# Seven of eight row-tile pairs in seven products, with the sums of weight blocks on POOL

## The chip, the cores and the metric

The kernel runs on one core of one Trainium2 chip. The metric is the device time of one execution in microseconds, the median of the runs shown. The engines are named as in the profile: PE (matrix products; PEld its weight loads), DVE (elementwise on vectors), ACT (activations and copies), POOL (GpSimd), SP (whose queue issues nearly all DMAs).

## The reference

The program is a two-layer decoder trunk over 256 tokens of 2048 features, in float32. Layer 0 mixes tokens with an mLSTM, layer 1 with an RG-LRU; behind each mixer comes a SwiGLU feed-forward block, which is the part that the change touches:

```python
D_MODEL = 2048; SEQ = 256; DEPTH = 2
D_FF = ((8 * D_MODEL // 3 + 255) // 256) * 256        # 5632

def swiglu(x, w_in, w_out):
    g, u = jnp.split(x @ w_in, 2, axis=-1)
    return (jax.nn.silu(g) * u) @ w_out

    h = x
    for layer in range(DEPTH):
        h = h + mixer(rms_norm(h, norm_mix[layer]), ...)
        h = h + swiglu(rms_norm(h, norm_ffn[layer]), ffn_w_in[layer], ffn_w_out[layer])
    return rms_norm(h, norm_final)
```

`ffn_w_in[layer]` is 2048 x 11264, `ffn_w_out[layer]` 5632 x 2048.

## The kernel before

**Split numbers.** A float32 product is made from three matmuls on a faster type (`fp32r`): every operand is split into a rounded part hi and a rest lo = x - hi, and hi*hi + hi*lo + lo*hi is accumulated in PSUM. For each weight block ACT makes hi by a cast and DVE makes lo by a subtraction whose two inputs (the raw weights and hi) lie in SBUF (`split`, `halves`, L267 to L269 and L243, L244 elsewhere). `product` (L818 to L821) issues the three matmuls, each 128 x 128 by 128 x 512.

**Blocks and pairs.** A feed-forward layer goes over 11 column blocks `j` of 512 gate and 512 up columns. Within a block it goes over eight pairs `p` of row tiles (2 x 128 rows of the weights). A pair of row tiles, two column halves (gate and up) and two token blocks of 128 form a 2 x 2 by 2 x 2 block product. The plain form takes eight products (24 matmuls). For the pairs in `SEVENS` a Strassen form with seven products (21 matmuls) is used, with results gathered in seven PSUM banks named P1, P2, Q3, Q5, P7, Q6, P4. It needs three raw weight blocks (B21, B11, B22, the tile called x) and four sums of weight blocks (T1, T3, T2, T4, the tile called t). In block 0 the pairs in `BOTH` are plain too.

**One pair of weights** (`pairs`, L293 to L318): SP issues two 512 KB loads into a raw tile of four 512-wide blocks. For a seven-product pair DVE makes the sums in a single buffer `sum` (L312: two blocks at once, 1024 wide; L315 and L316: one block each). ACT casts x (`whix`, 1536 wide) and t in two halves (`whit`, 1024 wide), DVE makes `wlox` and `wlot`. Three raw buffers and three hi and three lo buffers take turns; x and t of a pair take one hi and one lo buffer each, a plain pair takes one of each.

**Output.** The result of a block goes through L853 to L868 (copies, sums of banks, SiLU, product of gate and up; every bank must be read before the next block restarts it), is transposed into the banks P7 and Q6, and is multiplied with `ffn_w_out` in eight pieces of 12 matmuls. From block 1 on, `between` (L889 on) puts one such piece into each pair, a few products before its end, for the block before. Its weights (`rawo`, `whio`, `wloo`) are loaded by SP and split like the others, in 16 half blocks of 512 columns as eight pieces of 1024.

**Order.** Every engine runs its own queue in order. The order within a queue comes from the program's order and from `high_priority(offset=AHEAD)`, which moves weight splits ahead of what the program has just written; `pool_of(...).tile(..., tag=...)` gives a buffer, and whoever takes it again waits for its last reader.

Of the kernel before, what the change touches and what calls it, by code (L numbers as in the profile page):

```python
# [26 lines left out]
BIG = 1e30  # L27
AHEAD = 1000

SEVENS = (1, 2, 3, 4, 5, 6)  # L30

BOTH = (1, 2, 3, 4)

# [2 lines left out]
    ("P1", "A11", "B11"), ("P2", "A12", "B21"), ("Q3", "A3", "B22"),  # L36
    ("Q5", "A5", "T1"), ("P7", "A7", "T3"), ("Q6", "A6", "T2"), ("P4", "A22", "T4"),
)
SEVEN = ("A12", "A22", "A11", "A5", "A7", "A6", "A3")


@with_exitstack
def kernel(
# [38 lines left out]
    def pool_of(key):  # L82
        return pools[key][0]
# [73 lines left out]
    for i in range(9):  # L157
        nc.tensor.matmul(pwarm[:, 0:P], lhsT=ones, rhs=ones, start=True, stop=True)
    mhalf = const.tile([P, 2], F32, name="mhalf")
    nc.vector.memset(mhalf, -0.5)  # L160
    mask = const.tile([P, P], F32, name="mask")
    nc.gpsimd.memset(mask, 0.0)
    nc.gpsimd.affine_select(
        out=mask, in_=mask, compare_op=ALU.is_ge, fill=BIG, base=0,
        pattern=[[1, P]], channel_multiplier=-1,
    )


    par_src = [
# [55 lines left out]
    def stream(w, c0, nk, ncols=NB):  # L225
# [23 lines left out]


    PLACES = (
        "raw1", "raw2", "sum0", "rawo", "whio", "wloo", "wlo1", "whi1", "wlo2", "whi2", "raw0", "whi0", "wlo0",
    )
    turn, early = {}, {}

# [15 lines left out]
    def halves(name, src, n=4, step=4):  # L271

        hi, lo = four("whi", name, F32R, 3), four("wlo", name, F32R, 3)
        for i in range(0, n, step):
            at = slice(i, min(n, i + step))
            split(hi[:, at, :], lo[:, at, :], src[:, at, :])
        return [(hi[:, i, :], lo[:, i, :]) for i in range(n)]

    def stream4(w, c0, nk):

        wv = w.rearrange("(k p) n -> p k n", p=P)
        for kg in range(0, nk, 4):
            raw = four("raw", kg, F32, 3)
            for i in (0, 2):
                nc.sync.dma_start(raw[:, i:i + 2, :], wv[:, kg + i:kg + i + 2, c0:c0 + NB])
            with tc.high_priority(offset=AHEAD):
                both = halves(kg, raw)
            for i in range(4):
                yield kg + i, *both[i]

    def is_plain(j, p):
        return p not in SEVENS or j == 0 and p in BOTH

    def pairs(w, j, held):

        wv = w.rearrange("(k p) n -> p k n", p=P)
        for p in range(NK // 2):
            raw = four("raw", f"{j}_{p}", F32, 3)
            if held and j == 0 and p == 0:

                nc.vector.tensor_copy(raw[0:1, 0, 0:1], h[0:1, NT - 1, 2 * NB - 1:2 * NB])
            for i, c0 in enumerate((j * NB, FF + j * NB)):
                nc.sync.dma_start(raw[:, 2 * i:2 * i + 2, :], wv[:, 2 * p:2 * p + 2, c0:c0 + NB])
            if is_plain(j, p):
                with tc.high_priority(offset=AHEAD):
                    both = halves(f"{j}_{p}", raw)
                yield p, both
                continue

            with tc.high_priority(offset=AHEAD):  # L310
                t = four("sum", f"{j}_{p}", F32, 1)
                nc.vector.tensor_tensor(  # L312
                    t[:, 0:2, :], raw[:, 1:3, :], raw[:, 3:4, :].broadcast_to([P, 2, NB]), op=ALU.add
                )
                nc.vector.tensor_tensor(t[:, 2, :], t[:, 0, :], raw[:, 2, :], op=ALU.add)  # L315
                nc.vector.tensor_tensor(t[:, 3, :], t[:, 2, :], raw[:, 0, :], op=ALU.add)  # L316
                both = halves(f"x{j}_{p}", raw, 3) + halves(f"t{j}_{p}", t, step=2)
            yield p, dict(zip(("B21", "B11", "B22", "T1", "T3", "T2", "T4"), both))  # L318

# [45 lines left out]
    class Norm:  # L365
# [9 lines left out]
        def __init__(self, name, gain, bcast=False):  # L375
            self.name, self.gain, self.bcast, self.made = name, gain, bcast, []
            self.x = []
            self.ss = small.tile([P, NT, 4], F32, tag="ss", name=f"ss_{name}")

        def stats(self, q, blocks=range(NT)):  # L380
            for b in blocks:
                junk = self.scrap
                if junk is None:
                    junk = small.tile([P, NB], F32, tag="junk", name="junk", bufs=1)
                nc.scalar.activation(
                    junk, h[:, b, q * NB:(q + 1) * NB], AF.Square,
                    accum_out=self.ss[:, b, q:q + 1],
                )
# [47 lines left out]
        def finish(self):  # L436
            v = small.tile([P, NT], F32, tag="ms", name=f"ms_{self.name}")
            nc.vector.tensor_reduce(out=v, in_=self.ss, axis=mybir.AxisListType.X, op=ALU.add)
            nc.vector.tensor_scalar(out=v, in0=v, scalar1=1.0 / D, scalar2=EPS, op0=ALU.mult, op1=ALU.add)
            self.rstd = small.tile([P, NT], F32, tag="rstd", name=f"rstd_{self.name}")  # L440
            nc.gpsimd.tensor_tensor(self.rstd, v, mhalf[:, 0:NT], op=ALU.pow)
            if self.bcast:
                dg = small.tile([P, NT, P], F32, tag="dg", name=f"dg_{self.name}", bufs=1)
                for b in range(NT):
                    nc.vector.tensor_scalar_mul(dg[:, b, :], ident, self.rstd[:, b:b + 1])
                pb = misc(f"bc_{self.name}")
                nc.tensor.matmul(pb[:, 0:T], lhsT=ones, rhs=dg.rearrange("p b t -> p (b t)"), start=True, stop=True)
                self.bc = small.tile([P, T], F32, tag="rbc", name=f"rbc_{self.name}")
                nc.scalar.copy(self.bc, pb[:, 0:T])

    class NormPairs(Norm):


        def __init__(self, *args, **kw):
            super().__init__(*args, **kw)
            self.more = {}

        def pair(self, p):
            plain = p not in SEVENS
# [109 lines left out]
    def mlstm_mixer():  # L569
        mx = open_pool("mx", "mx", 2)  # L570
        if True:
            w = m_w_in[0]
            sel = mx.tile([H, H, P], F32R, name="sel", bufs=1)
            nc.gpsimd.tensor_copy(sel, ident[0:H, 0:H].unsqueeze(2).broadcast_to([H, H, P]))

            gw = mx.tile([P, NK, 2 * H], F32, name="gw", bufs=1)
            gwx = mx.tile([P, NK, 2, 2 * H], F32R, name="gwx", bufs=1)
            gsel = mx.tile([4 * H, 2 * H], F32, name="gsel", bufs=1)
# [132 lines left out]
            def head_out(j, a, vs, hn):  # L711
                hd = 2 * j + a
                for b in range(NT):
                    pv = misc(f"pv{hd}_{b}")
                    o = pv[:, 0:DV + 1]
                    if b == 0:
                        nc.tensor.matmul(o, lhsT=pw[hd][:, 0:P], rhs=vs[:, 0, a, :], start=True, stop=True)
                    else:
                        nc.tensor.matmul(o, lhsT=pw[hd][:, P:2 * P], rhs=vs[:, 0, a, :], start=True, stop=False)
                        nc.tensor.matmul(o, lhsT=pw[hd][:, 2 * P:3 * P], rhs=vs[:, 1, a, :], start=False, stop=True)  # L720
                    den = mx.tile([P, 4], F32, tag="den", name="den", bufs=4)
                    nc.vector.tensor_scalar(
                        out=den[:, 1:2], in0=pv[:, DV:DV + 1], scalar1=-1.0,
                        scalar2=ucol[:, 3 + b, hd:hd + 1], op0=ALU.mult, op1=ALU.max,
                    )
                    nc.vector.tensor_tensor(den[:, 0:1], pv[:, DV:DV + 1], den[:, 1:2], op=ALU.max)
                    nc.vector.reciprocal(den[:, 0:1], den[:, 0:1])
                    nc.vector.tensor_scalar_mul(hn[:, b, a, :], pv[:, 0:DV], den[:, 0:1])
                    junk = small.tile([P, NB], F32, tag="junk", name="junk", bufs=1)
                    nc.scalar.activation(junk[:, 0:DV], hn[:, b, a, :], AF.Square, accum_out=den[:, 1:2])  # L730
                    nc.vector.tensor_scalar(
                        out=den[:, 2:3], in0=den[:, 1:2], scalar1=1.0 / DV, scalar2=EPS,
                        op0=ALU.mult, op1=ALU.add,
                    )
                    nc.gpsimd.tensor_tensor(den[:, 3:4], den[:, 2:3], mhalf[:, 0:1], op=ALU.pow)
                    nc.gpsimd.tensor_scalar_mul(hn[:, b, a, :], hn[:, b, a, :], den[:, 3:4])
# [61 lines left out]
    def ffn(layer, n, nxt):  # L798
# [24 lines left out]
        def inner(j, between):  # L823
# [12 lines left out]
            for p, ops in pairs(w, j, layer == 1):  # L836
                if is_plain(j, p):

                    work = [
                        (c, n.plain(p, f)[a], ops[2 * side + f], p == NP - 1 and f == 1)  # L840
                        for c, side, a in (("Q5", 1, 1), ("P2", 0, 0), ("Q3", 1, 2), ("P4", 0, 1)) for f in range(2)
                    ]
                else:
                    seven = n.seven(p)
                    work = [
                        (c, seven[a], ops[b], p == SEVENS[-1] and c in ("P7", "P1", "Q6")) for c, a, b in PRODUCTS
                    ]
                for i, job in enumerate(work):
                    add(*job)
# [278 lines left out]
    class Final(Norm):  # L1128
# [9 lines left out]

        def mean(self, q, b, src):

            junk = small.tile([P, NB], F32, tag="junk", name="junk", bufs=1)
            nc.scalar.activation(junk, src, AF.Square, scale=D ** -0.5, accum_out=self.ss[:, b, q:q + 1])

        def scaled(self, q, b):
            cs = slice(q * NB, (q + 1) * NB)
# [63 lines left out]
```

## Time and profile before

| | before |
|---|---|
| median of 3 runs | 2085.85 us (2085.57 to 2086.32) |
| profiled execution | 2085.02 us, span 2083.2 us |
| granted PE clock | 0.999 |
| PE busy | 2069.3 us (99% of the span) |
| DVE busy | 1742.1 us (84%) |
| ACT busy | 1343.0 us (64%) |
| POOL busy | 43.2 us (2%) |
| sums on DVE (L312, L315, L316), 124 pairs | 151.5 + 85.3 + 85.2 us busy |
| DMA | 405.75 MB, mean 195 GB/s |

A row of the groups reads: line, engine, operation, out<-in by the program's names, shapes, count, then busy time in us, mean ns of one, and the idle time of the engine just before with what ended it. In a timeline row the first two numbers are the start and the duration in us, and what stands in brackets at its end is the engine's idle time before it. Durations of matmuls overlap, so PE's busy share says that it rarely stops, not what a matmul costs. The rest of the 2085 us outside the two feed-forward stages (about 395 to 1090 us and 1385 to 2083 us) is the mixers.

### The profile page before, as it was taken

What the parts mean: (1) busy time and instruction counts of PE and PEld (TensorE: products, weight loads), DVE (VectorE), ACT (ScalarE), POOL (GpSimd) and SP (SyncE); (2) the same over time, 40 slices, a digit from 0 to 9 for tenths busy, and PEclk for the clock granted to TensorE, in tenths of its full rate; (3) what the DMA queues carried; (4) which work ended last, traced back from release to release, by engine and by line L of the source; (5) the groups of instructions that cost most, each with busy time, mean ns of one, the idle gap of its engine ahead of it and who ended that gap; (6) DMA issues with size and microseconds to landing.
All of it is one profiled execution on the core that took longest, in us unless ns stands there. A gap on an engine that the chain in (4) does not pass through costs nothing.

```text
span 2083.2 us, 27536 instructions
## 1 busy us (share of the span) xinstructions
PE 2069.3 (99%) x10484; PEld 1752.6 (84%) x10484; DVE 1742.1 (84%) x1898; ACT 1343.0 (64%) x1627; POOL 43.2 (2%) x62
## 2 busy tenths in 40 slices
PE   9999999999999999999999999999999999999998
PEld 8988888887888888888889999888788888888886
DVE  6655556699999999999976787679999999999995
ACT  6344446566777676777764768556676776776774
POOL 0011110000000000000000000000000000000002
PEclk9999999999999999999999999999999999999999
DMA  7555656555665566565555665655556556566653
GB/s 229 171 162 177 178 181 222 190 173 200 206 215 198 192 216 208 200 216 192 185 179 161 192 187 189 219 207 181 201 204 222 195 186 208 201 211 212 202 188 135
DMA packets 211901, 405.75 MB, mean 195 GB/s; under 512 B 15080, under 2 KB 15800, under 8 KB 211640
## 3 DMA queue, kind: packets, MB, share of 16 engines
q1 hardware_dynamic: 211048, 402.92, 58.5%
q8 instruction: 82, 1.34, 0.3%
q10 hardware_dynamic: 720, 1.07, 0.1%
q14 instruction: 51, 0.42, 0.1%
HBM read 401.84 MB, written 2.10 MB: 194 GB/s over the span
## 4 chain that ended last, share of the span: by engine, by line
PE 93%; DVE 4%; ACT 1%; issue 1%; DMA 1%; POOL 0%; ACTq 0%; POOLq 0%; SPq 0%; DVEq 0%
PE P L820 7%; PE P L821 7%; PE out L819 7%; PE P L819 7%; PE out L821 7%; PE out L820 7%; PE Q L820 6%; PE Q L821 6%; PE Q L819 6%; PE po L330 3%; PE po L328 3%; PE po L329 3%; PE o L330 1%; PE v L328 1%; PE rec L347 1%; PE v L329 1%
## 5 line engine op out<-in xcount | busy, mean ns | idle before, releaser
L244 DVE TENSOR_TENSOR wlo<-raw,whi 128x1024 fp32r<-128x1024 f32 (+1 forms) x226 | 273.4, 1213 | 171.4 <-ACT whi L243 170.8
L243 ACT CAST whi<-raw 128x1024 fp32r<-128x1024 f32 (+1 forms) x226 | 234.7, 1043 | 196.7 <-PE po L330 43.3
L268 ACT CAST whit<-sum 128x1024 fp32r<-128x1024 f32 x248 | 255.1, 1052 | 145.0 <-DVE sum L316 79.4
L269 DVE TENSOR_TENSOR wlot<-sum,whit 128x1024 fp32r<-128x1024 f32 x248 | 297.2, 1220 | 20.0 <-ACT whit L268 20.0
L819 PE MATMUL out<-whio,hh 128*128 128x512 f32 x704 | 275.1, 391 | 0.1
L820 PE MATMUL out<-wloo,hh 128*128 128x512 f32 x704 | 274.1, 389 | 0.0
L821 PE MATMUL out<-whio,hh 128*128 128x512 f32 x704 | 273.9, 389 | 0.0
L269 DVE TENSOR_TENSOR wlox<-raw,whix 128x1536 fp32r<-128x1536 f32 x124 | 217.3, 1753 | 12.1 <-ACT whix L268 12.1
L268 ACT CAST whio<-rawo 128x1024 fp32r<-128x1024 f32 (+1 forms) x166 | 183.5, 1106 | 64.3 <-PE out L821 54.7
L269 DVE TENSOR_TENSOR wloo<-rawo,whio 128x1024 fp32r<-128x1024 f32 (+1 forms) x166 | 209.8, 1283 | 3.0 <-ACT whio L268 2.5
L268 ACT CAST whix<-raw 128x1536 fp32r<-128x1536 f32 x124 | 184.0, 1484 | 38.5 <-PE P L821 16.1
L938 ACT COPY h<-out 128x512 f32<-128x512 f32 x154 | 89.9, 584 | 126.1 <-PE out L821 125.8
L312 DVE TENSOR_TENSOR sum<-raw 128x1024 f32<-128x1024 f32 x124 | 151.5, 1222 | 7.0 <-DMA raw<-in_ffn_w_in_dram 2.6
L819 PEld LDWEIGHTS out<-whio,hh 128*128 128x128 f32 x704 | 132.1, 188 | 29.6 <-ACT out L927 1.8
L821 PEld LDWEIGHTS out<-whio,hh 128*128 128x128 f32 x704 | 132.1, 188 | 27.8
L820 PEld LDWEIGHTS out<-wloo,hh 128*128 128x128 f32 x704 | 132.2, 188 | 27.2
L269 DVE TENSOR_TENSOR wlo<-raw,whi 128x2048 fp32r<-128x2048 f32 x52 | 117.5, 2288 | 28.8 <-ACT whi L268 28.8
L268 ACT CAST whi<-raw 128x2048 fp32r<-128x2048 f32 x52 | 97.4, 1911 | 24.0 <-DMA raw<-in_ffn_w_in_dram 17.7
L819 PE MATMUL P<-whix,p_f 128*128 128x512 f32 x248 | 97.6, 399 | 1.8 <-ACT whix L268 1.8
L819 PE MATMUL Q<-whit,p_f 128*128 128x512 f32 x248 | 97.2, 392 | 0.8 <-ACT whit L268 0.8
L927 ACT COPY out<-h 128x512 f32<-128x512 f32 x156 | 91.9, 589 | 8.3 <-DVE h L936 6.7
L820 PE MATMUL P<-wlox,p_f 128*128 128x512 f32 x248 | 97.1, 391 | 0.2
(293 smaller groups left out, 5023.5 us busy)
## 6 DMA issues: line engine op xcount, KB each, us to landing
raw<-in_ffn_w_in_dram SPq DMA_DIRECT2D x352, 512.0 KB, 4.5
rawo<-in_ffn_w_out_dram SPq DMA_DIRECT2D x176, 512.0 KB, 4.9
raw<-in_m_w_in_dram SPq DMA_DIRECT2D x94, 512.0 KB, 3.7
raw<-in_r_w_in_dram SPq DMA_DIRECT2D x64, 512.0 KB, 4.4
raw<-in_m_w_out_dram SPq DMA_DIRECT2D x32, 512.0 KB, 3.8
raw<-in_r_w_out_dram SPq DMA_DIRECT2D x32, 512.0 KB, 4.3
gr<-in_r_gate_w_dram SPq DMA_DIRECT2D x8, 512.0 KB, 3.7
out_dram<-y SPq DMA_DIRECT2D x4, 512.0 KB, 3.0
```

The lines of the kernel that those rows point to most:

```text
L243: nc.scalar.copy(hi[:, i:i + step, 0:ncols], r)
L244: nc.vector.tensor_tensor(lo[:, i:i + step, 0:ncols], r, hi[:, i:i + step, 0:ncols].bitcast(F32), op=ALU.subtract)
L268: nc.scalar.copy(hi, src)
L269: nc.vector.tensor_tensor(lo, src, hi.bitcast(F32), op=ALU.subtract)
L312: nc.vector.tensor_tensor(t[:, 0:2, :], raw[:, 1:3, :], raw[:, 3:4, :].broadcast_to([P, 2, NB]), op=ALU.add)
L328: nc.tensor.matmul(o, lhsT=ah[:, bs], rhs=hi, start=(k == 0), stop=False)
L329: nc.tensor.matmul(o, lhsT=ah[:, bs], rhs=lo, start=False, stop=False)
L819: nc.tensor.matmul(o, lhsT=a[0], rhs=b[0], start=start, stop=False, **kw)
L820: nc.tensor.matmul(o, lhsT=a[0], rhs=b[1], start=False, stop=False, **kw)
L821: nc.tensor.matmul(o, lhsT=a[1], rhs=b[0], start=False, stop=stop, **kw)
L927: nc.scalar.copy(o, hs)
L938: nc.scalar.copy(hs, o)
```

## The change

`SEVENS` gains pair 7, so that only pair 0 stays plain from block 1 on. The sums move from DVE to POOL (`nc.gpsimd`), and are kept in half buffers of two blocks each: three of them take turns (`sums`; two in the place `sum0`, one in the new place `sum1`), and a pair uses two. Pair 7 goes through its seven products in the order `LAST`, since all seven banks now end there. The causal mask, the scratch tile `junk` and the tiles of the broadcast norm move into pools that are open only part of the time.

```diff
-SEVENS = (1, 2, 3, 4, 5, 6)
+SEVENS = (1, 2, 3, 4, 5, 6, 7)
...
+LAST = tuple(sorted(PRODUCTS, key=lambda c: ("P1", "Q6", "P7", "Q5", "P2", "Q3", "P4").index(c[0])))
...
     PLACES = (
-        "raw1", "raw2", "sum0", "rawo", "whio", "wloo", "wlo1", "whi1", "wlo2", "whi2", "raw0", "whi0", "wlo0",
+        "raw1", "raw2", "sum0", "rawo", "whio", "wloo", "wlo1", "whi1", "wlo2", "whi2", "raw0", "whi0", "wlo0", "sum1",
     )
...
-            split(hi[:, at, :], lo[:, at, :], src[:, at, :])
+            split(hi[:, at, :], lo[:, at, :], src[i // step] if isinstance(src, list) else src[:, at, :])
...
+    def sums(name):
+        at = turn.get("sum", 0)
+        turn["sum"] = (at + 1) % 3
+        return pool_of(f"sum{at // 2}").tile([P, 2, NB], F32, tag=f"sum{at}", name=f"sum{name}")
...
             with tc.high_priority(offset=AHEAD):
-                t = four("sum", f"{j}_{p}", F32, 1)
-                nc.vector.tensor_tensor(
-                    t[:, 0:2, :], raw[:, 1:3, :], raw[:, 3:4, :].broadcast_to([P, 2, NB]), op=ALU.add
-                )
-                nc.vector.tensor_tensor(t[:, 2, :], t[:, 0, :], raw[:, 2, :], op=ALU.add)
-                nc.vector.tensor_tensor(t[:, 3, :], t[:, 2, :], raw[:, 0, :], op=ALU.add)
+                t = [sums(f"{j}_{p}{i}") for i in range(2)]
+                nc.gpsimd.tensor_tensor(t[0], raw[:, 1:3, :], raw[:, 3:4, :].broadcast_to([P, 2, NB]), op=ALU.add)
+                nc.gpsimd.tensor_tensor(t[1][:, 0, :], t[0][:, 0, :], raw[:, 2, :], op=ALU.add)
+                nc.gpsimd.tensor_tensor(t[1][:, 1, :], t[1][:, 0, :], raw[:, 0, :], op=ALU.add)
                 both = halves(f"x{j}_{p}", raw, 3) + halves(f"t{j}_{p}", t, step=2)
...
                     seven = n.seven(p)
                     work = [
-                        (c, seven[a], ops[b], p == SEVENS[-1] and c in ("P7", "P1", "Q6")) for c, a, b in PRODUCTS
+                        (c, seven[a], ops[b], p == SEVENS[-1])
+                        for c, a, b in (LAST if p == SEVENS[-1] else PRODUCTS)
                     ]
```

**DVE, pairs 3 and 4 of a block in the first feed-forward layer.** Names end in the pair and a serial number. Before, the sums stand between the splits:

```order
L269 TENSOR_TENSOR wloo_8013<-rawo_8011,whio_8012 128x1024
L312 TENSOR_TENSOR sum_3_8047<-raw_3_8044 128x1024
L269 TENSOR_TENSOR wloo_8019<-rawo_8017,whio_8018 128x1024
L315 TENSOR_TENSOR sum_3_8047<-sum_3_8047,raw_3_8044 128x512
L269 TENSOR_TENSOR wlox_3_8052<-raw_3_8044,whix_3_8051 128x1536
L316 TENSOR_TENSOR sum_3_8047<-sum_3_8047,raw_3_8044 128x512
L269 TENSOR_TENSOR wlot_3_8056<-sum_3_8047,whit_3_8055 128x1024 x2
L312 TENSOR_TENSOR sum_4_8100<-raw_4_8097 128x1024
L315 TENSOR_TENSOR sum_4_8100<-sum_4_8100,raw_4_8097 128x512
L316 TENSOR_TENSOR sum_4_8100<-sum_4_8100,raw_4_8097 128x512
L269 TENSOR_TENSOR wlox_4_8105<-raw_4_8097,whix_4_8104 128x1536
```

The same place on DVE after the change:

```order
L265 TENSOR_TENSOR wlox_3_8183<-raw_3_8174,whix_3_8182 128x1536
L265 TENSOR_TENSOR wlot_3_8187<-sum_30_8177,whit_3_8186 128x1024
L265 TENSOR_TENSOR wlot_3_8187<-sum_31_8178,whit_3_8186 128x1024
L265 TENSOR_TENSOR wlox_4_8237<-raw_4_8228,whix_4_8236 128x1536
L265 TENSOR_TENSOR wlot_4_8241<-sum_40_8231,whit_4_8240 128x1024
L265 TENSOR_TENSOR wlot_4_8241<-sum_41_8232,whit_4_8240 128x1024
L265 TENSOR_TENSOR wloo_8263<-rawo_8261,whio_8262 128x1024
L265 TENSOR_TENSOR wloo_8269<-rawo_8267,whio_8268 128x1024
```

Only splits are left on DVE here, one behind the other, all of them with two inputs in SBUF.

**POOL, the first feed-forward layer.** Before, its queue goes from the norm's power (L441) straight to the next mixer:

```order
L735 TENSOR_TENSOR den<-den,mhalf 128x1
L736 TENSOR_SCALAR hn_2676<-hn_2676,den 128x256
L441 TENSOR_TENSOR rstd_f_3774<-ms_f_3771,mhalf 128x2
L1017 MEMSET rc_9188 128x4x3
L1017 MEMSET rc_9835 128x4x3
```

After the change the sums of all pairs stand in between, three operations a pair (`sum_30` and `sum_31` are the two half buffers of pair 3):

```order
L314 TENSOR_TENSOR sum_30_6659<-raw_3_6656 128x1024
L315 TENSOR_TENSOR sum_31_6660<-sum_30_6659,raw_3_6656 128x512
L316 TENSOR_TENSOR sum_31_6660<-sum_31_6660,raw_3_6656 128x512
L314 TENSOR_TENSOR sum_40_6713<-raw_4_6710 128x1024
L315 TENSOR_TENSOR sum_41_6714<-sum_40_6713,raw_4_6710 128x512
L316 TENSOR_TENSOR sum_41_6714<-sum_41_6714,raw_4_6710 128x512
```

The three additions of a pair moved from DVE's queue to POOL's, in the same order, each reading what the one before it wrote.

More of the change, by code (lines that the diff above doesn't have):

```diff
@@ L160 @@
     nc.vector.memset(mhalf, -0.5)
[L161 to L165, printed above, removed]
-    )
     par_src = [
@@ L310, in pairs @@
             with tc.high_priority(offset=AHEAD):
-                t = four("sum", f"{j}_{p}", F32, 1)
-                nc.vector.tensor_tensor(
-                    t[:, 0:2, :], raw[:, 1:3, :], raw[:, 3:4, :].broadcast_to([P, 2, NB]), op=ALU.add
-                )
-                nc.vector.tensor_tensor(t[:, 2, :], t[:, 0, :], raw[:, 2, :], op=ALU.add)
-                nc.vector.tensor_tensor(t[:, 3, :], t[:, 2, :], raw[:, 0, :], op=ALU.add)
+                t = [sums(f"{j}_{p}{i}") for i in range(2)]
+                nc.gpsimd.tensor_tensor(t[0], raw[:, 1:3, :], raw[:, 3:4, :].broadcast_to([P, 2, NB]), op=ALU.add)
+                nc.gpsimd.tensor_tensor(t[1][:, 0, :], t[0][:, 0, :], raw[:, 2, :], op=ALU.add)
+                nc.gpsimd.tensor_tensor(t[1][:, 1, :], t[1][:, 0, :], raw[:, 0, :], op=ALU.add)
                 both = halves(f"x{j}_{p}", raw, 3) + halves(f"t{j}_{p}", t, step=2)
@@ L378, in __init__, with junk @@
             self.ss = small.tile([P, NT, 4], F32, tag="ss", name=f"ss_{name}")
+        def junk(self):
+            return pool_of("x").tile([P, NB], F32, tag="junk", name="junk")
         def stats(self, q, blocks=range(NT)):
@@ L383, in stats @@
                 if junk is None:
-                    junk = small.tile([P, NB], F32, tag="junk", name="junk", bufs=1)
+                    junk = self.junk()
                 nc.scalar.activation(
@@ L442, in finish @@
             if self.bcast:
-                dg = small.tile([P, NT, P], F32, tag="dg", name=f"dg_{self.name}", bufs=1)
+                dg = pool_of("x").tile([P, NT, P], F32, tag="dg", name=f"dg_{self.name}")
                 for b in range(NT):
@@ L447, in finish @@
                 nc.tensor.matmul(pb[:, 0:T], lhsT=ones, rhs=dg.rearrange("p b t -> p (b t)"), start=True, stop=True)
-                self.bc = small.tile([P, T], F32, tag="rbc", name=f"rbc_{self.name}")
+                self.bc = pool_of("x").tile([P, T], F32, tag="rbc", name=f"rbc_{self.name}")
                 nc.scalar.copy(self.bc, pb[:, 0:T])
@@ L456, in __init__, with junk @@
             self.more = {}
+        def junk(self):
+            place, tag = ("c", "junk") if "c" in pools else ("rawo", "raw1")
+            return pool_of(place).tile([P, NB], F32, tag=tag, name="junk")
         def pair(self, p):
@@ L574, in mlstm_mixer @@
             nc.gpsimd.tensor_copy(sel, ident[0:H, 0:H].unsqueeze(2).broadcast_to([H, H, P]))
+            mask = mx.tile([P, P], F32, name="mask", bufs=1)
+            nc.gpsimd.memset(mask, 0.0)
+            nc.gpsimd.affine_select(
+                out=mask, in_=mask, compare_op=ALU.is_ge, fill=BIG, base=0,
+                pattern=[[1, P]], channel_multiplier=-1,
+            )
             gw = mx.tile([P, NK, 2 * H], F32, name="gw", bufs=1)
@@ L728, in head_out @@
                     nc.vector.tensor_scalar_mul(hn[:, b, a, :], pv[:, 0:DV], den[:, 0:1])
-                    junk = small.tile([P, NB], F32, tag="junk", name="junk", bufs=1)
-                    nc.scalar.activation(junk[:, 0:DV], hn[:, b, a, :], AF.Square, accum_out=den[:, 1:2])
+                    junk = mx.tile([P, DV], F32, tag="junk", name="junk", bufs=1)
+                    nc.scalar.activation(junk, hn[:, b, a, :], AF.Square, accum_out=den[:, 1:2])
                     nc.vector.tensor_scalar(
@@ L1139, in mean @@
         def mean(self, q, b, src):
-            junk = small.tile([P, NB], F32, tag="junk", name="junk", bufs=1)
-            nc.scalar.activation(junk, src, AF.Square, scale=D ** -0.5, accum_out=self.ss[:, b, q:q + 1])
+            nc.scalar.activation(self.junk(), src, AF.Square, scale=D ** -0.5, accum_out=self.ss[:, b, q:q + 1])
         def scaled(self, q, b):
```

## The prediction

> **What bounds the kernel now.** I read the page's busy shares first, then the chain that ended last, then busy time by stretches.
>
> ```profile
> PE 2069.3 (99%) x10484; PEld 1752.6 (84%) x10484; DVE 1742.1 (84%) x1898; ACT 1343.0 (64%) x1627; POOL 43.2 (2%) x62
> PE 93%; DVE 4%; ACT 1%; issue 1%; DMA 1%; POOL 0%; ACTq 0%; POOLq 0%; SPq 0%; DVEq 0%
> 455.00:490.00 35.00, 32.91 (x136) 24.35 (x135) 33.57 (x32) 21.74 (x22) 0.00 (x0) 1.00 0.58 194
> 500.00:600.00 100.00, 100.00 (x451) 82.99 (x450) 96.16 (x93) 69.04 (x78) 0.00 (x0) 1.00 0.58 198
> ```
>
> The columns of the last two rows are PE, PEld, DVE, ACT and POOL busy time, then granted clock, DMA share and GB/s. PE sets the pace (93% of the chain). In the feed-forward stage, though, DVE works 96 us of every 100, and POOL not at all; around 455 to 490 us DVE has nothing left and PE loses 2.1 us. So there are two limits close together, and the change touches both.
>
> What does one matmul cost? Not the 391 ns of the groups: matmuls overlap, and consecutive starts count.
>
> ```profile
> 700.17 0.39 PE L819 MATMUL P<-whix,p_f 128*128 128x512 f32 x1
> 700.40 0.39 PE L820 MATMUL P<-wlox,p_f 128*128 128x512 f32 x1
> 700.62 0.39 PE L821 MATMUL P<-whix,p_f 128*128 128x512 f32 x1
> 700.85 0.39 PE L819 MATMUL P<-whix,p_f 128*128 128x512 f32 x1
> ```
>
> Three starts in 0.68 us: 0.227 us each, 0.68 us for one product. The length of a column block is the distance of the ACT copy that stands once in each:
>
> ```profile
> 432.95 0.58 ACT L853 COPY ds<-P 128x512 f32<-128x512 f32 x1
> 731.21 0.58 ACT L853 COPY ds<-P 128x512 f32<-128x512 f32 x1
> 793.30 0.58 ACT L853 COPY ds<-P 128x512 f32<-128x512 f32 x1
> 1041.68 0.58 ACT L853 COPY ds<-P 128x512 f32<-128x512 f32 x1
> 1418.49 0.58 ACT L853 COPY ds<-P 128x512 f32<-128x512 f32 x1
> 2027.09 0.58 ACT L853 COPY ds<-P 128x512 f32<-128x512 f32 x1
> ```
>
> A steady block takes 62.09 us (270 matmuls are 61.2 us, the eight transposes the rest). From the last pair of block 0 to the last pair of block 10 the two feed-forward layers take 608.7 and 608.6 us. These stretches are the ground of the sum.
>
> **The change, part by part.** *PE.* Pair 7 falls from eight products to seven in 22 blocks: 22 x 0.68 = 15.0 us less. A steady block needs 61.4 us of PE.
>
> *DVE.* Per seven-product pair it loses the sums (L312, L315, L316); per block, pair 7 needs the x and t splits in place of one plain split.
>
> ```profile
> L269 DVE TENSOR_TENSOR wlot<-sum,whit 128x1024 fp32r<-128x1024 f32 x248 | 297.2, 1220 | 20.0 <-ACT whit L268 20.0
> L312 DVE TENSOR_TENSOR sum<-raw 128x1024 f32<-128x1024 f32 x124 | 151.5, 1222 | 7.0 <-DMA raw<-in_ffn_w_in_dram 2.6 <-issue 1.2 <-DVE ds L854 1.0
> 735.84 2.29 DVE L269 TENSOR_TENSOR wlo<-raw,whi 128x2048 fp32r<-128x2048 f32 x1
> 738.04 0.69 DVE L854 TENSOR_TENSOR ds<-Q,ds 128x512 f32<-128x512 f32 x1
> 743.31 1.75 DVE L269 TENSOR_TENSOR wlox<-raw,whix 128x1536 fp32r<-128x1536 f32 x1
> 744.98 0.68 DVE L864 TENSOR_TENSOR ds<-Q,ds 128x512 f32<-128x512 f32 x1
> 745.58 1.22 DVE L269 TENSOR_TENSOR wloo<-rawo,whio 128x1024 fp32r<-128x1024 f32 x1
> 746.71 0.68 DVE L865 TENSOR_TENSOR ds<-P,ds 128x512 f32<-128x512 f32 x1
> 747.31 0.74 DVE L868 SCALAR_TENSOR_TENSOR ds<-ds,rstd_f 128x512 f32<-128x512 f32 x1
> 747.97 1.22 DVE L269 TENSOR_TENSOR wloo<-rawo,whio 128x1024 fp32r<-128x1024 f32 x1
> ```
>
> From start to start: x split 1.67, a 1024-wide split 1.14 (the t halves have the same shape as wloo, 1.22 against 1.22 in mean), plain split 2.20, L868 0.66, each about 0.08 less than its span. A pair's sums took 1.14 and two 512-wide additions of 0.60 (as L864), 2.34 us, and are gone. DVE alone would then need 7 x 3.95 for x and t, 2.20 for pair 0, 8 x 1.14 for the output weights, 1.32 for L868 and some 5 for the reads of banks: 46 us of a 61-us block, ample by itself.
>
> *POOL.* It gets three additions per pair, 146 pairs in all. Does it run beside DVE? The few POOL rows of this trace decide the forecast.
>
> ```profile
> L1147 POOL TENSOR_TENSOR y<-h,gf x6: 1287/1300/3280, 2060.4 to 2074.0; 128x512 f32<-128x512 f32 x6
> 2060.44 2.55 POOL L1147 TENSOR_TENSOR y<-h,gf 128x512 f32<-128x512 f32 x2 [671.97 <-DVE h L936]
> 2062.97 2.28 DVE L269 TENSOR_TENSOR wloo<-rawo,whio 128x2048 fp32r<-128x2048 f32 x1
> 2063.13 3.28 POOL L1147 TENSOR_TENSOR y<-h,gf 128x512 f32<-128x512 f32 x1
> L735 POOL TENSOR_TENSOR den<-den,mhalf x16: 537/567/1389, 146.8 to 294.8; 128x1 f32<-128x1 f32 x16
> 247.01 1.22 DVE L244 TENSOR_TENSOR wlo<-raw,whi 128x1024 fp32r<-128x1024 f32 x1 [0.79 <-ACT whi L243]
> 247.28 1.39 POOL L735 TENSOR_TENSOR den<-den,mhalf 128x1 f32<-128x1 f32 x1
> 242.44 0.93 POOL L736 TENSOR_SCALAR hn<-hn,den 128x256 f32<-128x256 f32 x1
> 243.04 1.22 DVE L244 TENSOR_TENSOR wlo<-raw,whi 128x1024 fp32r<-128x1024 f32 x1
> ```
>
> Alone, a two-input 128x512 operation takes POOL 1.30 us (1.26 from start to start). The one that began 0.16 us into a DVE subtraction with both inputs in SBUF took 3.28 us: it ended 1.16 us after DVE's end at 2065.25. The 1-wide operation at 247.28, otherwise 0.57, took 1.39 and ended 0.44 behind DVE's end at 248.23. So POOL stands still while DVE subtracts from SBUF; DVE kept its 2.28 and 1.22. The other order, a two-input POOL operation under way when such a DVE operation comes, is in no row. The nearest is L736, with one tensor input: DVE began at 243.04, before its end at 243.37, and neither was longer than usual.
>
> I therefore take the two as users of something that one has at a time, and have to price POOL's hold. Upper end: the whole 1.26 us for 512 and 2.52 for 1024, 5.04 per pair. Lower end: the span without the last 0.33 us that did not stop DVE in L736, and without the 0.14 us that a held operation has done before its release (1.30 - 1.16): 0.83 for 512, 3.32 per pair. No row is nearer to one end than to the other, so I take the middle: 1.05 for 512, 2.10 for 1024, 4.2 per pair. DVE's own holds per pair are 1.67 + 2 x 1.14 + 1.14 (the 16 half blocks of the output weights are eight pieces of 1024 per block, one per pair) = 5.09. Three POOL operations also break DVE's run three times, and each break costs the 0.08 of overlap: 0.24.
>
> Block: 7 x (5.09 + 4.2 + 0.24) + (pair 0 with its output piece 2.20 + 1.14, two L868 1.32) = 71.4 us, against 61.4 on PE and 62.09 before. The pace passes from PE to DVE and POOL together. Ten blocks, less the five output pieces that block 1 and the cut leave out (5.7), are 708 us: 99 us longer than 608.7, in two layers 199. The last pair of each layer keeps its gain (1.4).
>
> [...]
>
> *ACT* gains pair 7's x and two t casts per block for one plain cast.
>
> ```profile
> L268 ACT CAST whit<-sum 128x1024 fp32r<-128x1024 f32 x248 | 255.1, 1052 | 145.0 <-DVE sum L316 79.4
> L268 ACT CAST whix<-raw 128x1536 fp32r<-128x1536 f32 x124 | 184.0, 1484 | 38.5 <-PE P L821 16.1
> L268 ACT CAST whi<-raw 128x2048 fp32r<-128x2048 f32 x52 | 97.4, 1911 | 24.0 <-DMA raw<-in_ffn_w_in_dram 17.7
> ```
>
> That is 1.48 + 2 x 1.05 - 1.91 = 1.7 us more in a block, on an engine that is busy 69 us in 100: hidden. Its t casts now wait for POOL and stand in front of the casts for the next pair and of the output weights; DVE's t splits wait for those casts, and its next x split stands behind them. A late sum thus stops both queues, which is why POOL's time is not hidden behind a long queue.
>
> *SP.* A raw buffer is released by POOL's last sum as well as by the x split; the loads behind it in SP's queue, output weights among them, wait with it.
>
> ```profile
> raw<-in_ffn_w_in_dram SPq DMA_DIRECT2D x352, 512.0 KB, 4.5
> ```
>
> Three buffers turn and a load can go out nearly two pairs ahead (a pair with its output piece is 33 matmuls, 7.5 us) against 4.5 us to land, so I cost it nothing; a longer period only gives it more room. Without that cover a load would be late by what POOL is late, which the block's sum holds already.
>
> *End of a block.* Bank Q5 must be read before pair 0 of the next block restarts it.
>
> ```profile
> 738.25 0.39 PE L819 MATMUL Q<-whi,p_f 128*128 128x512 f32 x1
> 740.98 1.22 DVE L859 TENSOR_TENSOR ds<-Q,ds 128x1024 f32<-128x1024 f32 x1
> 745.73 0.39 PE L819 MATMUL Q<-whi,p_f 128*128 128x512 f32 x1
> ```
>
> Now Q5's last product begins at 738.25, DVE reads it from 740.98 to 742.2, and PE comes back at 745.73: 3.5 us to spare. After the change 21 matmuls (4.8 us) lie between instead of 30 (6.8 us): 1.5 us to spare with today's DVE. DVE's slack covers it; if that is gone it is gone because POOL holds the pace, and then PE waits anyway. The moved mask, junk and broadcast buffers, and the four small subtractions that the seven-product form of pair 7 adds once per layer, cost under 1 us each and lie beside PE work: nothing.
>
> Sum: profiled execution 2085.0 + 199 - 1.4 = 2282.6; the median of the runs is 0.8 higher than that execution, so 2283 us. With POOL's low hold and no breaks a block is 63.5 us and the time 2126; with the high hold 77.3 us and 2401.
>
> **The rivals.** *POOL is free once begun (the other side).* If DVE does not stop for a POOL operation in flight, and that operation goes on, the sums disappear beside DVE. For it: L736 and L244 overlapped for 0.33 us at no cost. Against it: 3.28 us at 2063.13, and four of the 16 L735. Then PE keeps the pace: 2085.9 - 15.0, and half of the 2 x 2.1 us that PE loses near 455 and in the second layer: 2069 us. It decides when POOL's hold per pair falls to (61.4 - 4.7 - 1.7) / 7 - 5.09 = 2.8 us, 0.7 for a 512-wide operation.
>
> *They share by halves.* The hold is short of 0.83 but not nothing, because POOL uses only some cycles. Between the two cases: 2069 to 2126 us, 2095 as its middle.
>
> *The shorter end of the block bites alone.* POOL runs free, but DVE reaches the Q5 read 2 us later than the 1.5 us spare allows: 0.5 us in each of 20 blocks, 10 of the 17 us gone, 2079 us. DVE's 15 us of slack per block speak against it; I count it with the free case.
>
> **How the numbers follow.** One at a time: 0.68, giving 2126 to 2401, predicted 2283. Shared by halves: 0.14, mostly slower. Free: 0.18, faster. A difference of 0.2%, 4 us, is about what a measurement of this kernel can tell from no change. Faster: 0.18 and 0.03 of the shared case, 0.21; within 0.2%: 0.03; slower: 0.76. The likeliest case has the range 2126 to 2401. The range for 8 in 10 takes in the shared case from 2075 on and leaves out the free one: 2075 to 2401.
>
> **What would show it.** Right: POOL busy in most of each feed-forward slice, its 1024-wide additions well over 2.5 us where DVE subtracts; PE at 85 to 90% there; ACT's t casts idle until POOL; the L853 copies (then L867) about 71 us apart; a plain DVE split longer than 1.22 us in many places. Wrong: POOL additions of 1.3 and 2.5 us throughout and copies 61.4 us apart. That would say that the held operations in this trace were held only because they came second, and that POOL mostly comes first.

## The result, and the profile after

The changed kernel takes 2344.06 us (median of 5 runs, 2343.75 to 2344.64) against 2086.2 us for the kernel before (5 runs, 2085.57 to 2086.96): 1.1236 times as long, with a 95% interval of 1.122 to 1.1253. The forecast was 2283 us, slower, with a range of 2075 to 2401.

The page's busy row, its POOL slices and its chain, after the change:

```profile
PE 2136.1 (91%) x10418; PEld 1737.8 (74%) x10418; DVE 2011.2 (86%) x1576; ACT 1380.2 (59%) x1671; POOL 1158.6 (49%) x500
POOL 0011100678777776678700000067767787767872
PE 43%; DVE 24%; issue 17%; POOL 10%; ACT 5%; DMA 1%; DVEq 0%; POOLq 0%; ACTq 0%; SPq 0%
```

DVE lost 322 instructions and gained 269 us of busy time. POOL is busy for about three quarters of a feed-forward slice, and PE has fallen from 93% of the chain to 43%. The copy that stands once in each block (L853 before, L867 now; first and last of the first layer and three in a row of its middle):

```profile
441.67 0.58 ACT L867 COPY ds<-P 128x512 f32<-128x512 f32 x1
732.77 0.58 ACT L867 COPY ds<-P 128x512 f32<-128x512 f32 x1
807.12 0.58 ACT L867 COPY ds<-P 128x512 f32<-128x512 f32 x1
881.48 0.58 ACT L867 COPY ds<-P 128x512 f32<-128x512 f32 x1
1178.91 0.57 ACT L867 COPY ds<-P 128x512 f32<-128x512 f32 x1
```

A steady block is 74.36 us instead of 62.09. The ten blocks between the first and the last row take 737.2 us instead of 608.7: 128.5 us more. In the second layer it is 737.7 instead of 608.6, 129.1 more. Together these are the 258 us of the loss.

What in a block takes longer? One block, engine by engine (PE, PEld, DVE, ACT, POOL), and DVE's groups in it:

```profile
807.12:881.48 74.36, 64.94 (x276) 50.08 (x275) 72.93 (x41) 45.60 (x52) 54.30 (x21) 1.00 0.53 170
L265 DVE TENSOR_TENSOR wlot<-sum,whit 128x1024 fp32r<-128x1024 f32 x15 | 25.2, 1706 | 0.1
L265 DVE TENSOR_TENSOR wlox<-raw,whix 128x1536 fp32r<-128x1536 f32 x7 | 22.2, 3166 | 1.2 <-ACT whix L264 1.2
L265 DVE TENSOR_TENSOR wloo<-rawo,whio 128x1024 fp32r<-128x1024 f32 x8 | 18.1, 2290 | 0.0
L265 DVE TENSOR_TENSOR wlo<-raw,whi 128x2048 fp32r<-128x2048 f32 x1 | 3.4, 3368 | 0.0
L882 DVE SCALAR_TENSOR_TENSOR ds<-ds,rstd_f 128x512 f32<-128x512 f32 x2 | 1.5, 738 | 0.0
L547 DVE TENSOR_TENSOR hh<-tv,hh 128x512 fp32r<-128x512 f32 x2 | 1.3, 678 | 0.0
L873 DVE TENSOR_TENSOR ds<-Q,ds 128x1024 f32<-128x1024 f32 x1 | 1.2, 1212 | 0.0
```

DVE is hardly ever idle (72.93 of 74.36 us), yet it has less work than before: the same instructions last longer. The 1536-wide split went from 1.75 to 3.17 us, the 1024-wide ones from 1.22 to 1.71 and 2.29. Those that read a PSUM bank and one SBUF tile did not move: L547 stayed at 0.68 us, though 36 of its 44 instances had a POOL addition beside them. (L873 never had one, and L882, which has two inputs in SBUF, had none in this block, so these two rows say nothing.) On POOL the same picture (min, median and max of the additions):

```profile
L314 POOL TENSOR_TENSOR sum<-raw x146: 2384/3377/3933, 410.5 to 2280.9; 128x1024 f32<-128x1024 f32 x146
L315 POOL TENSOR_TENSOR sum<-sum,raw x146: 1285/2151/2161, 413.4 to 2284.4; 128x512 f32<-128x512 f32 x146
L316 POOL TENSOR_TENSOR sum<-sum,raw x146: 1277/2152/3229, 414.8 to 2286.6; 128x512 f32<-128x512 f32 x146
```

Side by side, DVE's and POOL's timelines show how they take turns:

```profile
797.90 4.53 DVE L265 TENSOR_TENSOR wloo<-rawo,whio 128x1024 fp32r<-128x1024 f32 x2
799.21 2.14 POOL L316 TENSOR_TENSOR sum<-sum,raw 128x512 f32<-128x512 f32 x1
801.31 3.37 POOL L314 TENSOR_TENSOR sum<-raw 128x1024 f32<-128x1024 f32 x1
802.35 3.94 DVE L265 TENSOR_TENSOR wlox<-raw,whix 128x1536 fp32r<-128x1536 f32 x1
806.22 2.35 DVE L265 TENSOR_TENSOR wlot<-sum,whit 128x1024 fp32r<-128x1024 f32 x2
812.98 2.40 POOL L314 TENSOR_TENSOR sum<-raw 128x1024 f32<-128x1024 f32 x1
813.21 3.26 DVE L265 TENSOR_TENSOR wloo<-rawo,whio 128x1024 fp32r<-128x1024 f32 x1
```

Two output splits take 4.45 us from start to start (797.90 to 802.35) where two took 2.28: 1.09 us went to one POOL addition of 512 each. The x split takes 3.87 instead of 1.67: 2.20 for the 1024-wide addition. The last two rows are the order that no row of before had. POOL came first, was done in its undisturbed 2.40 us at 815.38, and the DVE split that began 0.23 us after it ended at 816.47, 1.09 us behind POOL's end, when it needs 1.22. So all but 0.13 us of the split's work came behind POOL's recorded end.

Two waits show what hangs behind, PE's weight load behind DVE and ACT's cast behind POOL (us in total, times, longest):

```profile
ACT whit L264 <- POOL sum L316: 211.2, 118, 3.9
PEld out L833 <- DVE wloo L265: 128.3, 103, 2.1
```

### The profile page after: what moved, and what is told of

The parts are those of the page before. It is cut to its first block, busy times and chain, and to the rows that moved or that the text cites. A ratio compares the mean times of both kernels' runs of the same rounds, so it can differ in the third digit from the quotient of the medians.

```text
span 2342.0 us, 28166 instructions
## 1 busy us (share of the span) xinstructions
PE 2136.1 (91%) x10418; PEld 1737.8 (74%) x10418; DVE 2011.2 (86%) x1576; ACT 1380.2 (59%) x1671; POOL 1158.6 (49%) x500
## 4 chain that ended last, share of the span: by engine, by line
PE 43%; DVE 24%; issue 17%; POOL 10%; ACT 5%; DMA 1%; DVEq 0%; POOLq 0%; ACTq 0%; SPq 0%
DVE wloo L265 13%; DVE wlot L265 5%; POOL sum L316 5%; POOL sum L315 4%; DVE wlox L265 3%; PE po L328 2%; PE po L330 2%; PE po L329 2%; PE out L832 2%; PE out L833 2%; PE out L834 2%; ACT whit L264 2%; PE Q L833 2%; ACT whix L264 1%; PE Q L834 1%
## 5 line engine op out<-in xcount | busy, mean ns | idle before, releaser
L265 DVE TENSOR_TENSOR wlot<-sum,whit 128x1024 fp32r<-128x1024 f32 x292 | 507.3, 1763 | 1.7
L315 POOL TENSOR_TENSOR sum<-sum,raw 128x512 f32<-128x512 f32 x146 | 309.4, 2119 | 394.1 <-DVE wlot L265 286.6
L314 POOL TENSOR_TENSOR sum<-raw 128x1024 f32<-128x1024 f32 x146 | 476.5, 3263 | 19.8 <-DMA raw<-in_ffn_w_in_dram 17.5
L264 ACT CAST whit<-sum 128x1024 fp32r<-128x1024 f32 x292 | 303.8, 1049 | 292.2 <-POOL sum L316 211.2
L265 DVE TENSOR_TENSOR wlox<-raw,whix 128x1536 fp32r<-128x1536 f32 x146 | 447.4, 3065 | 32.3 <-ACT whix L264 32.3
L265 DVE TENSOR_TENSOR wloo<-rawo,whio 128x1024 fp32r<-128x1024 f32 (+1 forms) x166 | 356.6, 2174 | 29.6 <-ACT whio L264 29.3
L833 PE MATMUL out<-wloo,hh 128*128 128x512 f32 x704 | 287.7, 409 | 86.5 <-DVE wloo L265 85.4
L316 POOL TENSOR_TENSOR sum<-sum,raw 128x512 f32<-128x512 f32 x146 | 336.8, 2307 | 11.4
L264 ACT CAST whix<-raw 128x1536 fp32r<-128x1536 f32 x146 | 215.8, 1478 | 29.0 <-PE Q L834 19.6
L833 PE MATMUL P<-wlox,p_f 128*128 128x512 f32 x292 | 121.9, 417 | 53.8 <-DVE wlox L265 53.8
L833 PE MATMUL Q<-wlot,p_f 128*128 128x512 f32 x292 | 120.9, 414 | 32.9 <-DVE wlot L265 32.9
```

The source lines that it names most:

```text
L264: nc.scalar.copy(hi, src)
L265: nc.vector.tensor_tensor(lo, src, hi.bitcast(F32), op=ALU.subtract)
L314: nc.gpsimd.tensor_tensor(t[0], raw[:, 1:3, :], raw[:, 3:4, :].broadcast_to([P, 2, NB]), op=ALU.add)
L315: nc.gpsimd.tensor_tensor(t[1][:, 0, :], t[0][:, 0, :], raw[:, 2, :], op=ALU.add)
L316: nc.gpsimd.tensor_tensor(t[1][:, 1, :], t[1][:, 0, :], raw[:, 0, :], op=ALU.add)
L833: nc.tensor.matmul(o, lhsT=a[0], rhs=b[1], start=False, stop=False, **kw)
```

## The experiments

Theory: operations of POOL that read SBUF and operations of DVE with two inputs in SBUF exclude each other, whichever comes first, and a block lasts as long as the two together. Rivals: the loss lies in waiting for POOL's results and half buffers; or in the other parts of the change (seven products in pair 7, the later end of the banks, the moved buffers).

**Sums back on DVE.**

```diff
-                nc.gpsimd.tensor_tensor(t[0], ...)     # and the two behind it
+                nc.vector.tensor_tensor(t[0], ...)
```

> The changed kernel with its sums put back on DVE; seven products for pair 7, the order of its products, the half buffers and the moved scratch tiles stay. Theory (POOL's and DVE's operations with two inputs in SBUF exclude each other): the loss goes with POOL, and DVE alone is the limit: 45.6 + 7 x 2.34 = 62.0 us of DVE per block against 61.4 of PE and 62.09 before, so 2080 to 2105 us. Rival (seven products in pair 7, the later end of the banks or the moved buffers cost the time): stays near 2344 us.

Measured: 2106.83 us, 1.0105 times before (1.009 to 1.012). Of the 258 us that the change lost, 236 are gone with POOL alone. At 2106.83 us it ends 1.8 us above the range expected. What remains is the limit that DVE sets:

```profile
619.30:682.60 63.30, 62.15 (x276) 50.62 (x275) 61.97 (x61) 45.36 (x53) 0.00 (x0) 1.00 0.58 200
```

In this block DVE works 61.97 us, as worked out, but the block takes 63.30: a wait of 1.30 us in DVE's queue makes it slower than the 62.09 of before. The addition L314 waits there for a raw load; over the whole execution these waits are 19.7 us, and the run is 21.9 us slower than the kernel of before. Seven products in pair 7 are no gain this way either.

**Pair 7 plain, sums on POOL.** `SEVENS` is (1, ..., 6) again, and the last products stop as before.

> The changed kernel with pair 7 plain again (six pairs in seven products), the sums still on POOL. Theory: one seven-product pair's splits and sums (1.67 + 2.28 + some 4.6 us) leave the shared stretch of a block and one plain split (2.2) comes in, 74.35 - 6.3 = 68.0 us per block against 62.09: about 2205 us, still far slower than before. Rival (pair 7 is the cause): near 2086 us.

Measured: 2228.18 us, 1.0688 (1.0666 to 1.0709); 68.6 to 69.4 us per steady block, where 68.0 was expected, and 23 us above the 2205 expected in all. Apart from the moved scratch tiles this is the kernel of before with its sums on POOL, and it already loses 143 us. Pair 7 is not the cause; it is one more pair that pays.

**No sums.** The t splits read raw blocks; the sums are left out.

```diff
-                t = [sums(f"{j}_{p}{i}") for i in range(2)]
-                nc.gpsimd.tensor_tensor(...)           # all three
+                t = [raw[:, 0:2, :], raw[:, 2:4, :]]
```

> The changed kernel without the sums of weight blocks: the t splits read raw blocks instead, so POOL has no part in the feed-forward stage and the output is not the reference's. All theories: PE's gain shows alone, 22 products fewer, 15 us, and up to 4 us of the waits near the first blocks: 2067 to 2072 us. If it stays above 2080, the new end of a block (bank Q5 read later) costs what PE saves.

Measured: 2095.43 us, 1.0049 (1.0032 to 1.0065): outside what was expected. The steady blocks are 61.86 us, shorter than the 62.09 of before and the same as in the run with fills below, so the end of the block does not account for it. Most of the time is lost where a feed-forward stage begins. SP's queue, its waits from 370 to 415 us (the same wait stands once more ahead of the second stage):

```profile
SPq L305 <- PE po L327: 20.0, 1, 20.0
```

The first weight loads went out at 397.97 us, after the mixer's last products on PE, instead of 390.56 in the run with fills below. With the places for sums never used, the buffers probably came to lie elsewhere in SBUF, on tiles that the mixer still reads; that is inferred, not shown. The run is therefore no measure of PE's gain; the run with fills is nearer to one.

**Additions that nobody reads.** As above, and POOL adds a constant tile to itself, in the same three shapes, into the half buffers.

```diff
+                d = [sums(f"{j}_{p}{i}") for i in range(2)]
+                nc.gpsimd.tensor_copy(d[0][:, 0, 0:1], raw[:, 3, 0:1])
+                nc.gpsimd.tensor_tensor(wide, ones8, ones8, op=ALU.add)    # 1024, then twice 512
+                t = [raw[:, 0:2, :], raw[:, 2:4, :]]
```

> As the kernel without sums, but POOL makes the same three additions per pair (1024, 512 and 512 wide) from a constant tile into the half buffers, which nobody reads; one 1-wide copy from the raw tile per pair sets its pace. Theory (exclusion): DVE is slowed although it waits for no result, 7 x (5.09 + 4.6) + 4.7 = 72.5 us per block: 2300 to 2350 us. Rival (the loss is the wait for POOL's results and for its half buffers): 2067 to 2075 us.

Measured: 2186.29 us, 1.0487 (1.0466 to 1.0508), between the two expectations.

```profile
L317 POOL TENSOR_TENSOR sum<-ones x146: 1894/2764/3303, 411.5 to 2129.1; 128x1024 f32<-128x1024 f32 x146
L265 DVE TENSOR_TENSOR wlot<-raw,whit 128x1024 fp32r<-128x1024 f32 x292 | 523.7, 1831 | 0.2 <-ACT whit L264 0.2
```

DVE is slowed (1.83 us instead of 1.22) by a POOL for which nobody waits, so the rival cannot be the whole loss. But additions of a small constant tile to itself are cheaper, 1.89 us undisturbed against 2.38 for the sums, and so this run could not say how much of the rest is waiting.

**The real sums, unread.** POOL makes exactly the sums of the changed kernel; the t splits read raw blocks.

```diff
                 nc.gpsimd.tensor_tensor(t[1][:, 1, :], t[1][:, 0, :], raw[:, 0, :], op=ALU.add)
+                t = [raw[:, 0:2, :], raw[:, 2:4, :]]
```

> POOL makes exactly the sums of the changed kernel from the raw tiles, but the t splits read raw blocks, so nobody waits for a sum and no half buffer waits for a reader. Theory (exclusion; holds read from the changed kernel's trace: 1.13 us for 512 wide, 2.27 for 1024, 4.53 per pair; POOL never idle for a buffer, so it also covers DVE's reads of banks): 7 x (5.09 + 4.53) + 4.7 = 72.0 us per block, 2285 to 2320 us. If the waits for results carry most of the loss: below 2200 us.

Measured: 2340.88 us, 1.1226 (1.1205 to 1.1246): within 0.2% of the changed kernel. The loss needs no wait for a result: nobody waits for a sum, and it is as large. One block of this run shows DVE at work for 72.22 of 74.78 us (its operations undisturbed are 45.6 us). The 20 to 55 us less that I expected from a POOL free of its half buffers did not come; POOL waits for raw loads instead:

```profile
733.89:808.67 74.78, 67.09 (x277) 52.16 (x276) 72.22 (x40) 45.88 (x53) 51.07 (x21) 0.95 0.53 166
L314 POOL TENSOR_TENSOR sum<-raw 128x1024 f32<-128x1024 f32 x146 | 437.7, 2998 | 445.5 <-DMA raw<-in_ffn_w_in_dram 445.5
L265 DVE TENSOR_TENSOR wlot<-raw,whit 128x1024 fp32r<-128x1024 f32 x292 | 528.8, 1848 | 1.9 <-ACT whit L264 1.9
```

**Fills and copies in place of additions.** What about POOL is it that stops DVE? Four fills (no input) or four copies from the raw tile (one input) per pair, 1024 wide, unread.

```diff
+                    nc.gpsimd.memset(d[0], 0.0)                     # fills
+                    nc.gpsimd.tensor_copy(d[0], raw[:, 0:2, :])     # copies
```

> As the kernel without sums, but POOL fills the half buffers four times 1024 wide per pair with a constant (no input), about 4 us per pair; nobody reads them, a 1-wide copy from the raw tile per pair sets the pace. If DVE and POOL exclude each other only where both read SBUF: 2067 to 2075 us with DVE splits at 1.22 us. If any work of POOL stops DVE: 7 x 4 us more per block, about 2250 to 2300 us.

> As the run with unread fills, but POOL's four 1024-wide operations per pair are copies from the raw tile: one input in SBUF instead of none or two. If any POOL read excludes DVE's two-input operations: holds of some 0.9 us each, 7 x (5.09 + 3.6) + 4.7 = 65.5 us per block, about 2150 to 2180 us, and DVE splits well over 1.22 us. If only POOL operations with two inputs exclude them: 2067 to 2075 us.

Measured: fills 2073.09 us, 0.994 (0.9918 to 0.9963); copies 2167.34 us, 1.0393 (1.0374 to 1.0412). First the fills' groups, then those of the copies and pieces of both timelines:

```profile
L317 POOL MEMSET sum<- 128x1024 f32 x292 | 279.4, 957 | 315.7 <-DVE h L538 299.0
L265 DVE TENSOR_TENSOR wlot<-raw,whit 128x1024 fp32r<-128x1024 f32 x292 | 343.7, 1218 | 4.4 <-ACT whit L264 4.4
```

```profile
L315 POOL COPY sum<-raw x292: 1037/1915/2982, 409.6 to 2103.7; 128x1024 f32<-128x1024 f32 x146
L265 DVE TENSOR_TENSOR wlot<-raw,whit 128x1024 fp32r<-128x1024 f32 x292 | 543.7, 1900 | 0.8 <-ACT whit L264 0.8
800.03 4.03 DVE L265 TENSOR_TENSOR wlot<-raw,whit 128x1024 fp32r<-128x1024 f32 x2
803.99 4.04 DVE L265 TENSOR_TENSOR wloo<-rawo,whio 128x1024 fp32r<-128x1024 f32 x2
802.93 4.01 POOL L315 COPY sum<-raw 128x1024 f32<-128x1024 f32 x2
703.85 2.14 POOL L316 COPY sum<-raw 128x1024 f32<-128x1024 f32 x2
704.05 0.67 DVE L877 TENSOR_TENSOR ds<-P,ds 128x512 f32<-128x512 f32 x1
704.65 0.67 DVE L879 TENSOR_TENSOR ds<-Q,ds 128x512 f32<-128x512 f32 x1
```

Fills overlap freely, with DVE at its 1.22 us. Copies take turns with DVE's splits like additions: 3.96 us for two of each. So POOL's reading is what counts, with one input (1.90 us for a 1024-wide split beside the copies, instead of 1.22) or two (1.85 beside the unread sums). On DVE's side it is the operations with two inputs in SBUF: those with one input in a PSUM bank (L877, L879) ran in 0.67 us while POOL made two copies at its undisturbed pace. The run with fills also shows what the change is worth when POOL does not stop DVE: 11.7 us less than before, in blocks of 61.85 us. That is not PE's gain alone, since DVE is also rid of the sums there.

**Two half buffers instead of three.** `turn["sum"] = (at + 1) % 2`.

> The changed kernel with two half buffers in turn instead of three. If the sum of holds alone sets the pace: within 10 us of 2344. If how far POOL may run ahead matters too (in the changed kernel POOL stands idle for 9.45 us of a 74.35 us block, waiting for a half buffer while DVE and PE pass the plain pair): 2380 us or more.

Measured: 2356.54 us, 1.1304 (1.1271 to 1.1336); 74.1 to 74.9 us per steady block against 74.36. That lies between the two expectations. Before the first two additions of a pair POOL stands idle for 453 us in all, other than for loads, against 396 in the changed kernel, and the run is 12 us slower. The block is made up otherwise, though:

```profile
737.95:812.80 74.85, 67.83 (x278) 52.31 (x277) 65.95 (x40) 45.09 (x53) 52.41 (x22) 0.95 0.51 170
```

DVE is idle for 8.9 us of it, where it was idle for 1.4 in the changed kernel, and is stopped for some 20 us instead of 27. With two half buffers DVE's t splits wait 140.3 us in all for ACT's casts of the sums, against 1.7 in the changed kernel: waits have taken the place of a part of the stops. That the sum stays nearly the same is not explained by this run, so it does not show that POOL's lead is without effect.

**POOL for one pair only.**

```diff
+                on = nc.gpsimd if p == 1 else nc.vector
-                nc.gpsimd.tensor_tensor(t[0], ...)     # and the two behind it
+                on.tensor_tensor(t[0], ...)
```

> A try for a version that beats both: seven products in pair 7, sums on DVE except for pair 1, whose sums fall where DVE reads banks (5.3 us per block with at most one input in SBUF) and go to POOL. If POOL's 4.53 us of holds fall there: DVE 62.0 - 2.3 = 59.7 us per block, PE the limit at 61.4 to 61.9: 2070 to 2080 us. If they fall on the splits around it: 59.7 + 4.5 = 64.2 us per block, 2110 to 2130 us.

Measured: 2149.18 us, 1.0311 (1.0297 to 1.0325); steady blocks from 63.8 to 66.3 us: no better version, and beyond even the bad end of what was expected. POOL's additions did not fall where DVE reads banks:

```profile
L316 POOL TENSOR_TENSOR sum<-sum,raw x20: 2141/3200/3233, 440.0 to 2037.2; 128x512 f32<-128x512 f32 x20
```

Not one of the 20 ran undisturbed in 1.28 us: all of them met DVE's splits. What that does to a block:

```profile
691.32:756.51 65.19, 62.34 (x277) 50.63 (x275) 63.36 (x59) 45.44 (x53) 8.00 (x4) 1.00 0.58 194
```

DVE has 2.3 us of sums less to do than in the first experiment (59.6 us of the 61.97), yet is busy for 63.36 us: some 3.7 of the pair's 4.4 us of holds were paid, and the other 1.8 of the block's 65.2 are waits, against 1.3 in the first experiment. Why steady blocks differ by up to 2.5 us among themselves stays open. Nothing that was run beats the kernel of before and is also the whole computation.

## Why the prediction was right

*The verdict and its mechanism* stood as written: one user at a time, DVE's splits stretched, PE waiting in the feed-forward stage (busy for 64.94 of 74.36 us, 87%), the block longer than before (by 9.3 us in the forecast, by 12.3 as measured). The reading rested on four of the 16 L735 and one of the six L1147, which lasted too long in the trace of before.

*POOL's hold per pair.* Predicted 4.2 us and 0.24 for broken runs, 4.44 together; by start-to-start times 2.20 + 2 x 1.09 = 4.38. The middle between the two bounds was good, but no row of before spoke for it rather than for either end, so that it came this close is in part luck. The lower bound, taken from L736, was probably not a case of POOL coming first and letting DVE pass: the copies show that one-input reads exclude too (1.90 us for a split instead of 1.22), so L736 most likely no longer held DVE by then; no trace shows that, and that operation itself was not tried.

*The block.* Predicted 71.4 us, measured 74.36. The step that failed is "7 x (5.09 + 4.2 + 0.24) + pair 0 + L868", which leaves DVE's reads of banks (some 5.3 us) out of the sum without giving a reason. That is right only if POOL works all through them. DVE's operations at their undisturbed times are 45.6 us of the block (with the sums on DVE it came to 61.97, which is 45.6 + 7 x 2.34), and its idle time 74.36 - 72.93 = 1.4; the remaining 27.3 are stops. POOL's seven pairs hold 7 x 4.38 = 30.7 us, so only 3.4 us fell into the 6.7 us in which DVE left it alone. There POOL stood waiting, as these rows of the changed kernel show:

```profile
809.79 3.23 POOL L316 TENSOR_TENSOR sum<-sum,raw 128x512 f32<-128x512 f32 x1
812.98 2.40 POOL L314 TENSOR_TENSOR sum<-raw 128x1024 f32<-128x1024 f32 x1
824.83 2.12 POOL L315 TENSOR_TENSOR sum<-sum,raw 128x512 f32<-128x512 f32 x1 [9.45 <-ACT h L952]
```

From 815.38 to 824.83 POOL does nothing, while DVE reads the banks from 816.39 on. The profile names ACT's copy of `h` as what ended this wait, but the addition uses nothing of it; its half buffer comes free with a t split, and two of these began on DVE at 823.45, most likely the end of the wait. The 3 us missing per block, over some 20 blocks, are the 61 us between 2283 and 2344.

*One user at a time, in both orders.* The traces show both: 3.28 against 1.30 us for a POOL addition that came second (before, at 2063.13 us), and 3.26 against 1.22 us for a DVE split that did (changed kernel, at 813.21 us). A POOL operation that only wrote was free of it (1.22 us for DVE's splits beside the fills). The hold is a little shorter than POOL's whole span: a 1024-wide addition took 2.20 us out of DVE's x split, where its own undisturbed span is 2.40, and the split at 813.21 ended 1.09 us behind POOL where it needs 1.22.

*PE's gain.* Predicted 15.0 us and about 2069 us with POOL out of the way; the run with fills gave 2073.09. Its steady blocks are 61.85 us instead of 61.41, so they are only 0.24 us shorter than before, where the forecast had 0.68. The rest is a wait of about 0.4 us in each block at an output product that follows the block's last product (in one block it starts at 617.63, just after ACT's copy of `h` to `out` of 616.99 to 617.58), which I had costed at nothing. Some 20 steady blocks thus gave 4.8 of the 11.7 us; the other 7 came in the first and last blocks of the layers and were not followed up. That the total came within 4 us of 2069 is in part luck.

*ACT, SP, the end of the block, the moved buffers* were costed at nothing. In the run with fills the wait for ACT's copy is worth some 8.8 us (0.44 in each of 20 blocks); in the changed kernel PE has slack, and DVE is idle for only 1.4 us of a block, so little of theirs can be in it.

## What to carry to other kernels

Before work moves to POOL from a DVE that is nearly full, ask which of POOL's operations read SBUF and which of DVE's have two inputs there, and add up their times as if they were one engine: here a pair's additions took 2.20 + 2 x 1.09 us out of DVE's time. POOL was busy for 2% before, and that was no spare capacity here for sums of SBUF tiles beside a DVE at 84%. A few operations of unusual length in the old trace, set against what ran beside them, were enough to forecast a loss of 9% where 12% was measured. And time that one engine leaves free counts as cover only when the other has inputs and buffers at that moment: here 3.4 of 6.7 us of a block did.

## What was not expected of the hardware

PE's granted clock, 0.999 over the span before, fell to about half eleven times in the feed-forward stages of the changed kernel, nine times for 3.4 us and twice for 6.8. In the 3.4 us ahead of each fall PE had been busy for half of the time at most (0.01 to 0.50). A stretch inside such a fall, and two whole blocks, the first with one of these falls, the second without:

```profile
659.70:663.00 3.30, 3.06 (x7) 2.50 (x8) 3.30 (x2) 0.00 (x0) 3.22 (x2) 0.52 0.75 282
732.77:807.12 74.35, 65.92 (x276) 51.30 (x275) 71.14 (x41) 45.50 (x53) 54.28 (x21) 0.98 0.53 170
807.12:881.48 74.36, 64.94 (x276) 50.08 (x275) 72.93 (x41) 45.60 (x52) 54.30 (x21) 1.00 0.53 170
```

Both blocks last the same (74.35 and 74.36 us), so the slower clock cost nothing here: PE had slack, and the pace was set elsewhere. The falls came behind PE's waits.

DVE and POOL also took turns one operation at a time, with neither starved, although neither waited for the other's results (the run with copies, two of each in 3.96 us).
